# Last expert pair summed on TensorE inside the final layer norm, the last full expert unit moved ahead, and every low part of an expert weight made by VectorE

## The chip, the cores and the metric

The kernel runs on one core of one Trainium2 chip. The metric is device time in microseconds (us), from launch to end. A core has five engines with queues of their own: TensorE (PE in the rows, its weight loads PEld), VectorE (DVE), ScalarE (ACT), GpSimd (POOL) and SyncE (SP, which here only issues transfers). Each works through its queue in order, and semaphores tie the queues together.

## The reference

Two blocks of a model follow each other on 1024 tokens of width 1024. The change touches the end of the second: a mixture of 16 experts and the layer norm behind it.

```python
def grouped_moe(x, router_w, router_bias, w_gate, w_up, w_down):
    scores = jax.nn.sigmoid((xt @ router_w).astype(jnp.float32))
    # each token: the best group of experts, in it TOP_K = 2 experts, gates normalised
    ...
    def expert_block(args):
        xb, ei = args
        hb = jax.nn.silu(xb @ w_gate[ei]) * (xb @ w_up[ei])
        return hb @ w_down[ei]
    ...
    y = (yb[dest].reshape(T, TOP_K, D) * gate[..., None].astype(x.dtype)).sum(1)

# second_block, at its end
        ff = grouped_moe(x, router_w, router_bias, w_gate[l], w_up[l], w_down[l])
        x = layer_norm(DEEPNORM_ALPHA * x + ff, ln_moe_g[l], ln_moe_b[l])
```

## The kernel before

Tokens lie in eight tiles of 128 rows. After the cross attention each finished tile is stored three times (`tile`): as it is for the later gathers (`x2`, `x2a`), and times ALPHA into `acc`, a table in HBM on which the experts' results are added. `router` takes two tiles at a time: a long chain of small VectorE instructions picks the experts and counts rows, with a few TensorE products between (L2294 counts, L2368 places rows), and `table_a` and `table_b` write the row numbers for the gathers.

The experts' work comes in units (`experts`). A full unit (`full`, m = 0 to 15, here F0 to F15) gathers up to 128 rows of one expert, turns them, and multiplies in split precision: each fp32 matrix is cut into a high part (ScalarE, L2398) and a low part (L2401), and `mm3` makes three one-pass products (L336 to L338) of them. A half unit (`half`, H0 to H15) takes 64 further rows of an expert in plain fp32 (L2514 first matrix, L2538 second). Two half units share a gather and one result tile `yB`; H14 and H15 form the last pair, P7, H12 and H13 form P6. Every full unit and every pair ends in an indirect transfer from GpSimd's queue that adds its rows onto `acc` (L2379); these adds follow one another (`self.added`), since two of them may touch the same row.

An expert's weights are six tiles of 512 KB. Four go into general slots. The last two (`w` in the rows), those of the second matrix, go into a ring of two buffers for every expert but 0, 1 and 15: the next expert's two can be loaded only when full and half unit of this expert are done with them. So F14 and H14 wait for a load that itself waits for H13.

The order of all this is made by `Plan.run`: each step has an engine, a cost, a key and dependencies, and is issued to the engines' queues in the order in which the plan would start it. A step may name two engines; the plan takes the one that would end it sooner. The low part of a weight is such a step (`("dve", "pool"), (1.14, 2.3)` in `split`). Of 102 low parts 91 stand on VectorE and 11 on GpSimd.

When the plan is done, `rest` handles overflow (a loop that is not entered with these inputs). `finish_all` then loads the eight tiles of `acc` (L2705), all behind the last add, and norms them one after the other: mean and variance on VectorE (tiles 0, 2, 4, 6) or in two ScalarE passes (L2718, L2719; tiles 1, 3, 5, 7), the root on GpSimd, the rest on VectorE (L2730, L2739) or on ScalarE and GpSimd (L2736, L2737), and a store (L2740).

Of the kernel before, what the change touches and what calls it, by code (L numbers as in the profile page):

```python
# [9 lines left out]
F32 = mybir.dt.float32  # L10
F32R = mybir.dt.float32r
# [10 lines left out]
D = 1024  # L22
NT = 8
# [168 lines left out]
class K:  # L192
    def __init__(self, tc, nc, ctx, A):
        self.tc, self.nc, self.A = tc, nc, A
        P = lambda name, bufs, **k: ctx.enter_context(tc.tile_pool(name=name, bufs=bufs, **k))
        self.cp = P("const", 1)
        self.sp = P("slots", 41)
        self.xp = P("x", 3)
        self.wp = P("wts", 2)
        self.mp = P("small", 4)  # L200
        self.pp = P("psum", 2, space=PSUM)
# [294 lines left out]
def L(f, *a):  # L496
    return lambda *x: f(*a, *x)
# [1638 lines left out]
class Moe:  # L2136
# [253 lines left out]
    def split(self, plan, key, raw, W, c, slot, deps=(), room=()):  # L2390
        k, nc = self.k, self.k.nc

        def hi():
            if slot:
                W[c] = k.slot([128, 1024], F32R, "mh"), k.slot([128, 1024], F32R, "ml")
            else:
                W[c] = tuple(k.wp.tile([128, 1024], F32R, tag=t, name=k.nm(t)) for t in ("wh", "wl"))
            nc.scalar.copy(W[c][0], raw[c])  # L2398

        def lo(e):  # L2400
# [89 lines left out]
    def half(self, plan, key, m, x, raw, B, got, ready, done):  # L2490
# [76 lines left out]
        if v:  # L2567
            self.added = plan.op("pool+", 1.46, key, lambda: self.add(self.tb[0][:, p:p + 1], b0.pop("y")), b0["o"] + [self.added],
                                 free=["sl"])

    def table(self, acc, w, lo, hi, out):
        V, n = self.k.nc.vector, hi - lo
# [41 lines left out]
    def experts(self, plan, ld):  # L2614
# [61 lines left out]
        def norm():  # L2676
            self.fin = k.bcast(k.A["ln_moe_g"], D), k.bcast(k.A["ln_moe_b"], D)
        plan.op("sp+", 2.9, 126, norm, [began[13]], ["sl", "sl"])

    def blocks(self, plan, d):  # L2680

# [15 lines left out]
        plan.op("dve", 0.6, 110, count, [d], free=["pt"])  # L2697

    def finish_all(self, out):
        k = self.k  # L2700
        self.rest()
        ys, Z = {}, {}
        for i in range(NT):
            ys[i] = k.slot([128, 1024], name="fin")
            k.nc.sync.dma_start(out=ys[i], in_=self.acc[i * 128:(i + 1) * 128, :])  # L2705
        for i in range(NT + FIN_LAG):
            if i < NT:
                Z[i] = self.center(ys[i], i)
            if i >= FIN_LAG:
                self.finish(*Z.pop(i - FIN_LAG), i - FIN_LAG, out)  # L2710

    def center(self, y, i):

        k, nc, V = self.k, self.k.nc, self.k.nc.vector
        r, z = k.small([128, 1], "rstd"), k.slot([128, 1024], name="z")
        if i in FIN_ACT:
            mean, var = k.small([128, 1], "fs"), k.small([128, 1], "fv")
            nc.scalar.activation(z, y, AF.Copy, scale=-1.0 / D, accum_out=mean)  # L2718
            nc.scalar.activation(z, y, AF.Square, bias=mean, accum_out=var)  # L2719
            nc.gpsimd.tensor_scalar(r, var, 1.0 / D, LN_EPS, op0=OP.mult, op1=OP.add)  # L2720
            nc.gpsimd.tensor_tensor(r, r, k.mhalf[:, :1], op=OP.pow)
            op = OP.add
        else:
            st, mv = k.small([128, 2, 6], "bn"), k.small([128, 2], "mv")
            for h in range(2):
                V.bn_stats(st[:, h, :], y[:, h * 512:(h + 1) * 512])
            V.bn_aggr(mv, st.rearrange("p a b -> p (a b)"))
            k.rsqrt(r, mv[:, 1:2], LN_EPS)
            mean, op = mv[:, 0:1], OP.subtract
        V.scalar_tensor_tensor(z, y, mean, self.fin[0], op0=op, op1=OP.mult)  # L2730
        return z, r

    def finish(self, z, r, i, out):
        nc = self.k.nc
        if i in FIN_POOL:
            nc.scalar.activation(z, z, AF.Copy, scale=r)  # L2736
            nc.gpsimd.tensor_add(z, z, self.fin[1])  # L2737
        else:
            nc.vector.scalar_tensor_tensor(z, z, r, self.fin[1], op0=OP.mult, op1=OP.add)  # L2739
        nc.sync.dma_start(out=out[i * 128:(i + 1) * 128, :], in_=z)  # L2740


def build(tc, nc, A, ctx, outs, stop=None):
# [115 lines left out]
```

## Time and profile before

| what | value |
|---|---|
| time, median of 3 runs | 2333.01 us (2327.34 to 2335.35) |
| the profiled execution: its time, its span | 2338.79 us, 2337.0 us |
| busy share PE, PEld, DVE, ACT, POOL | 94%, 75%, 51%, 40%, 21% |
| mean granted TensorE clock | 0.975 |
| chain that ended last, whole span | PE 81%, DMA 7%, DVE 6%, ACT 2%, issue 2%, POOL 2% |
| the same chain, from 2050 us on, its costliest | DMA `acc<-yB,tab` 10.5%, PE L2514 9.7%, DMA `w<-w_moe` 9.6%, issue 7.4%, PE L2538 6.9%, DMA `acc<-my,tab` 5.6% |

The span is the time from the first to the last instruction; the profiled execution's own time is 1.8 us longer. [...] TensorE is nearly always busy until 2273 us and not at all from there to the end.

### The profile page before, as it was taken

What the parts mean: (1) busy time and instruction counts of PE and PEld (TensorE: products, weight loads), DVE (VectorE), ACT (ScalarE), POOL (GpSimd) and SP (SyncE); (2) the same over time, 40 slices, a digit from 0 to 9 for tenths busy, and PEclk for the clock granted to TensorE, in tenths of its full rate; (3) what the DMA queues carried; (4) which work ended last, traced back from release to release, by engine and by line L of the source; (5) the groups of instructions that cost most, each with busy time, mean ns of one, the idle gap of its engine ahead of it and who ended that gap; (6) DMA issues with size and microseconds to landing.
All of it is one profiled execution on the core that took longest, in us unless ns stands there. A gap on an engine that the chain in (4) does not pass through costs nothing.

```text
span 2337.0 us, 32698 instructions
## 1 busy us (share of the span) xinstructions
PE 2191.6 (94%) x12068; PEld 1746.3 (75%) x12068; DVE 1199.3 (51%) x2889; ACT 941.4 (40%) x1983; POOL 489.8 (21%) x629
## 2 busy tenths in 40 slices
PE   7999999999999999999999999998999998899880
PEld 7888778888777777777778898885778886666650
DVE  6323678833444444344444422787364456767544
ACT  5323677722444444444442222455101122455442
POOL 2000455300132222222300000211010013323114
PEclk9999999999999999999999999999999998999995
DMA  4112220322222221221353221229675135687855
GB/s 163 44 47 93 80 64 29 103 95 94 83 68 73 68 64 50 65 73 59 115 183 117 91 87 64 95 74 320 246 269 221 46 142 204 196 269 244 299 120 175
DMA packets 100257, 291.47 MB, mean 125 GB/s; under 512 B 12396, under 2 KB 25452, under 8 KB 100096
## 3 DMA queue, kind: packets, MB, share of 16 engines
q1 hardware_dynamic: 79072, 233.71, 28.8%
q0 software_dynamic: 6912, 25.17, 4.7%
q10 hardware_dynamic: 14112, 30.48, 4.1%
q8 instruction: 96, 1.57, 0.3%
q14 instruction: 65, 0.53, 0.1%
HBM read 206.92 MB, written 70.86 MB: 119 GB/s over the span
## 4 chain that ended last, share of the span: by engine, by line
PE 81%; DMA 7%; DVE 6%; ACT 2%; issue 2%; POOL 2%; SPq 0%; POOLq 0%; DVEq 0%; ACTq 0%
PE pd L336 15%; PE pd L338 14%; PE pd L337 14%; PE ps L336 4%; PE ps L338 4%; PE po L640 4%; PE ps L337 4%; PE ps L591 3%; PE pt L618 3%; PE pd L1898 2%; PE ps L986 2%; PE pd L2514 2%; PE po L1029 1%; DMA acc<-yB,tab 1%; DMA w<-w_moe 1%
## 5 line engine op out<-in xcount | busy, mean ns | idle before, releaser
L336 PE MATMUL pd<-fh,wh 128*128 128x512 f32 x880 | 353.7, 402 | 0.6 <-DVE st L1242 0.2
L338 PE MATMUL pd<-fh,wl 128*128 128x512 f32 x880 | 348.2, 396 | 0.5 <-DVE wl L314 0.5
L337 PE MATMUL pd<-fl,wh 128*128 128x512 f32 x880 | 347.7, 395 | 0.0
L336 PE MATMUL pd<-wh,fh 128*128 128x258 f32 (+3 forms) x616 | 202.0, 328 | 2.1 <-DVE n L1432 2.0
L337 PE MATMUL pd<-wl,fh 128*128 128x258 f32 (+3 forms) x616 | 200.9, 326 | 0.0
L338 PE MATMUL pd<-wh,fl 128*128 128x258 f32 (+3 forms) x616 | 200.5, 326 | 0.0
L336 PEld LDWEIGHTS pd<-fh,wh 128*128 128x128 f32 x880 | 165.4, 188 | 42.9 <-issue 7.1
L338 PEld LDWEIGHTS pd<-fh,wl 128*128 128x128 f32 x880 | 165.4, 188 | 40.0 <-issue 2.3
L337 PEld LDWEIGHTS pd<-fl,wh 128*128 128x128 f32 x880 | 165.6, 188 | 34.9 <-issue 0.2
L314 DVE TENSOR_TENSOR wl<-w,wh 128x1024 fp32r<-128x1024 f32 (+5 forms) x92 | 106.7, 1165 | 138.6 <-ACT wh L312 138.6
L312 ACT CAST wh<-w 128x1024 fp32r<-128x1024 f32 (+5 forms) x99 | 97.2, 990 | 140.9 <-PE pd L337 111.6
L626 ACT COPY PT<-pt 128x512 f32<-128x512 f32 (+2 forms) x192 | 86.3, 478 | 139.5 <-PE pt L618 139.1
L605 POOL TENSOR_SCALAR P<-P,rinv 128x256 f32<-128x256 f32 (+7 forms) x128 | 95.7, 748 | 192.8 <-DVE rinv L604 163.1
L602 ACT ACTIVATE P<-P,m 128x256 f32<-128x256 f32 (+7 forms) x128 | 99.6, 778 | 76.8 <-DVE m L596 75.7
L336 PEld LDWEIGHTS pd<-wh,fh 128*128 128x128 f32 x616 | 116.4, 189 | 13.3 <-DVE n L1432 2.7
L337 PEld LDWEIGHTS pd<-wl,fh 128*128 128x128 f32 x616 | 116.4, 189 | 9.9 <-issue 0.2
L338 PEld LDWEIGHTS pd<-wh,fl 128*128 128x128 f32 x616 | 116.3, 189 | 9.9
L1305 POOL TENSOR_TENSOR dm<-lcb,mask 128x128 f32<-128x128 f32 x128 | 60.4, 472 | 282.1 <-DVE m L596 227.3
L591 PE MATMUL ps<-st,st 128*128 128x512 f32 (+3 forms) x384 | 106.4, 371 | 1.0 <-DMA st<-st 0.6
L640 PE MATMUL po<-PT,V 128*64 128x256 f32 (+1 forms) x640 | 95.8, 371 | 0.0
L618 PE MATMUL pt<-ident,P 128*128 128x128 f32 x576 | 88.4, 276 | 3.6 <-POOL P L605 3.3
L596 DVE CUSTOM_DVE_ANT_0 P<-ps,lcb 128x512 f32<-128x512 f32 (+3 forms) x112 | 63.8, 570 | 48.3 <-PE ps L591 47.6
(499 smaller groups left out, 4730.9 us busy)
## 6 DMA issues: line engine op xcount, KB each, us to landing
mw<-w_moe SPq DMA_DIRECT2D x70, 512.0 KB, 7.0
w<-o_wc SPq DMA_DIRECT2D x30, 512.0 KB, 4.1
w<-w_moe SPq DMA_DIRECT2D x26, 512.0 KB, 5.1
xr<-xs SPq DMA_DIRECT2D x18, 512.0 KB, 4.6
s<-x_wkv SPq DMA_DIRECT2D x16, 512.0 KB, 5.7
lcb<-dn SPq DMA_DIRECT2D x16, 512.0 KB, 4.6
st<-st ACTq DMA_DIRECT2D x64, 128.0 KB, 2.4
wkd<-kvw SPq DMA_DIRECT2D x32, 256.0 KB, 2.7
```

What stands on the lines that cost most here:

```text
L312: nc.scalar.copy(hi[:, :n], raw[:, :n])
L314: (eng or nc.vector).tensor_sub(lo[:, :n], raw[:, :n], hi[:, :n].bitcast(F32))
L336: first = mm(out, lhs[0], rhs[0], start=start, stop=False)
L337: mm(out, lhs[0], rhs[1], start=False, stop=False)
L338: mm(out, lhs[1], rhs[0], start=False, stop=stop)
L591: ins = nc.tensor.matmul(ps[:, :m], l, r, start=t == 0, stop=t == len(passes) - 1)
L596: nc.vector.tensor_tensor_reduce(sb[:, c0:c0 + n0], ps[:, c0 - c:c0 - c + n0], b, -scale, acc, OP.add, OP.min, mx)
L602: nc.scalar.activation(sb[:, :w], sb[:, :w], AF.Exp, bias=acc, scale=-1.0, accum_out=sm)
L605: nc.gpsimd.tensor_scalar(sb[:, :w], sb[:, :w], ri, 0.0, op0=OP.mult, op1=OP.add)
L618: ins = nc.tensor.transpose(pt[:, j * 128:(j + 1) * 128], p[:, (c + j) * 128:(c + j + 1) * 128], k.ident)
L626: nc.scalar.copy(dst, src)
L640: st["V", n + i] = nc.tensor.matmul(o[a * 64:(a + 1) * 64, cols], val(a, j), PT[i // 2, a, j // 4][:, j % 4, n0:], start=j == 0, stop=j == ...
```

## The change

1. `finish_all` no longer finds the last pair in `acc`. P7's result `yB` stays on the chip (`self.last`), and the plan has no add for it. A new step `choose` builds `sel`, a matrix of ones and zeros that says which of its rows belongs to which token. `finish_all` cuts `yB` into high and low part, and for each of the eight tiles TensorE sums in PSUM: the identity times the loaded `acc` tile in plain fp32 (`sums`), and `sel` times the two parts (`pair`).
2. The norm reads that sum from PSUM. Only tile 0 takes its statistics from VectorE; tiles 1 to 7 take two ScalarE passes each. VectorE centres every tile (out of PSUM) and finishes it; GpSimd only makes the roots. The steps are ordered by a plan of their own, with room for four tiles in PSUM.
3. `MT_ORDER`: F15 stands ahead of H13, not behind it.
4. All low parts go to VectorE (cost 1.2 in the plan), none to GpSimd. As one step's cost and engine change, the plan issues everything behind the first of them in another order.

```diff
-MT_ORDER = ... [(v, m + 1 - v) for m in range(2, 15) for v in range(2)] + [(1, 15)]
+MT_ORDER = MT_ORDER[:-4] + [(0, 15), (1, 13), (1, 14), (1, 15)]
...
-FIN_ACT, FIN_POOL, FIN_LAG = (1, 3, 5, 7), (0, 1, 2, 4), 1
+FIN_ACT = range(1, 8)
...
-            (nc.vector, nc.gpsimd)[e].tensor_sub(W[c][1], raw[c], W[c][0].bitcast(F32))
+            nc.vector.tensor_sub(W[c][1], raw[c], W[c][0].bitcast(F32))
...
-        return plan.op(("dve", "pool"), (1.14, 2.3), key, lo, [d])
+        return plan.op("dve", 1.2, key, lo, [d])
...
+        if m == 15:
+            plan.op("-", 0, key, lambda: b0.update(last=b0.pop("y")), b0["o"])
+            self.last = b0
+        elif v:
             self.added = plan.op("pool+", 1.46, key, lambda: self.add(...), b0["o"] + [self.added], free=["sl"])
...
+    def choose(self):
+        ...
+        V.tensor_tensor(self.sel.rearrange("p (i t) -> p i t", i=8), self.iota.unsqueeze(1).to_broadcast([128, 8, 128]),
+                        t[:, 8:16].unsqueeze(2).to_broadcast([128, 8, 128]), op=OP.is_equal)
...
+        def sums(i):
+            PS[i] = banks.tile([128, 1024], F32, tag="sum", name=k.nm("sum"))
+            for n in range(2):
+                nc.tensor.matmul(PS[i][:, s(n)], k.ident, fin[i][:, s(n)], start=True, stop=False)
+        def pair(i, n):
+            for w in (yh, yl):
+                nc.tensor.matmul(PS[i][:, s(n)], self.sel[:, i * 128:(i + 1) * 128], w[:, s(n)], start=False, stop=w is yl)
+        def mean(i):
+            nc.scalar.activation(junk, PS[i], AF.Copy, scale=-1.0 / D, accum_out=T[i][0])
+        def var(i):
+            nc.scalar.activation(junk, PS[i], AF.Square, bias=T[i][0], accum_out=T[i][1])
+        def center(i):
+            V.scalar_tensor_tensor(Z[i], PS.pop(i), T[i][0] if i in FIN_ACT else T[i][:, 0:1], self.fin[0], ...)
+        def last(i):
+            V.scalar_tensor_tensor(Z[i], Z[i], R[i], self.fin[1], op0=OP.mult, op1=OP.add)
```

Where instructions stand now. First GpSimd's queue around the router of tiles 4 and 5 (`ml` and `wl` are low parts, `rstd` roots of the attention's norm, `xg` gathered rows), before:

```order
L370 TENSOR_TENSOR rstd_17478<-rstd_17478,mhalf 128x1
L2401 TENSOR_TENSOR ml_17590<-mw_17537,mh_17589 128x1024
L2401 TENSOR_TENSOR ml_17626<-mw_17539,mh_17625 128x1024
L2401 TENSOR_TENSOR ml_17629<-mw_17555,mh_17628 128x1024
L2401 TENSOR_TENSOR wl_17665<-mw_17584,wh_17664 128x1024
L369 TENSOR_SCALAR rstd_17724<-mv_17722 128x1
```

and VectorE's queue behind that router now (`rt` are the router's last small steps, `ptl` and `xr` belong to the attention, `tab` is the table for the gathers):

```order
L2367 TENSOR_TENSOR rt_17553<-rt_17553 128x4x24
L2072 TENSOR_TENSOR ptl_17643<-pt_17644,pth_17642 128x512
L2072 TENSOR_TENSOR ptl_17643<-pt_17657,pth_17642 128x512
L2404 TENSOR_TENSOR ml_17590<-mw_17537,mh_17589 128x1024
L2404 TENSOR_TENSOR ml_17625<-mw_17539,mh_17624 128x1024
L2088 SCALAR_TENSOR_TENSOR xr_17453<-xr_17453,pd_17665 128x512
L2375 TENSOR_TENSOR mcst_16088<-mcst_16088,po_17416 128x48
L2591 TENSOR_SCALAR tab_17731<-mcst_16088 128x16
```

The subtractions that stood on GpSimd while VectorE did the router's steps stand on VectorE behind those steps.

TensorE's queue at the end of the experts, before (weights `w_20088` belong to expert 13, `w_20147` to 14; the row of `w_19984` is H12, the `mid_20113` and `mid_20141` rows are H14 and H15, the `pd` rows their first matrix; `ps_20149` is F13, `ps_20168` F15, `ps_20215` F14):

```order
L2538 MATMUL ps_20074<-w_19984,mid_19804 64x512 x2
...
L2514 MATMUL pd_20083<-mw_19605,xbT_20037 64x256 x4
...
L2538 MATMUL ps_20136<-w_20088,mid_19843 64x512 x2
...
L336 MATMUL ps_20149<-wh_20121,ms_19875 128x512
...
L336 MATMUL ps_20168<-mh_19955,ms_20079 128x512
...
L2538 MATMUL ps_20200<-w_20147,mid_20113 64x512 x2
...
L2538 MATMUL ps_20206<-mw_19806,mid_20141 64x512 x2
...
L336 MATMUL ps_20215<-wh_20177,ms_19990 128x512
```

and now (`ps_20088` is F13, `w_19999` with `mid_19919` H13, `pd_20127` the first matrix of H14, `ps_20181` F15, `ps_20199` F14):

```order
L339 MATMUL ps_20088<-wh_20053,ms_19961 128x512
...
L2541 MATMUL ps_20119<-w_19999,mid_19919 64x512 x2
...
L2517 MATMUL pd_20127<-mw_19693,xbT_20079 64x256 x4
...
L339 MATMUL ps_20181<-mh_20009,ms_20117 128x512
...
L339 MATMUL ps_20199<-wh_20159,ms_20051 128x512
...
L2541 MATMUL ps_20223<-w_20132,mid_20155 64x512 x2
...
L2541 MATMUL ps_20229<-mw_19921,mid_20179 64x512 x2
```

H13 stands ahead of the last pair's first matrix, no longer behind it, and F14 stands ahead of H14 and H15, no longer last. GpSimd's queue of adds ended, before, with F13, F14, P6, F15 and P7:

```order
L2379 DMA acc<-my_20166,tab_17739 1152x1024
L2379 DMA acc<-my_20230,tab_17739 1152x1024
L2379 DMA acc<-yB_20090,tab_17739 1152x1024
L2379 DMA acc<-my_20187,tab_17739 1152x1024
L2379 DMA acc<-yB_20211,tab_17739 1152x1024
```

and ends now, behind P5, with F13, F14, F15 and P6:

```order
L2382 DMA acc<-yB_19668,tab_17731 1152x1024
L2382 DMA acc<-my_20106,tab_17731 1152x1024
L2382 DMA acc<-my_20214,tab_17731 1152x1024
L2382 DMA acc<-my_20197,tab_17731 1152x1024
L2382 DMA acc<-yB_20001,tab_17731 1152x1024
```

One add is gone, and two full units' adds stand directly behind each other.

## Rows read from the trace of the kernel before

**Rows 1.** Four stretches: length, busy us (instructions) per engine, granted clock, DMA share, GB/s
```profile
1944.00:1950.00 6.00, 6.00 (x21) 5.34 (x22) 5.62 (x28) 2.12 (x3) 0.00 (x0) 0.50 0.00 1
1999.00:2005.00 6.00, 6.00 (x18) 4.94 (x19) 5.25 (x25) 1.33 (x2) 0.00 (x0) 0.50 0.01 3
2012.00:2225.00 213.00, 198.54 (x1148) 139.59 (x1148) 138.55 (x192) 113.81 (x174) 52.84 (x35) 0.97 0.82 259
2300.00:2337.00 37.00, 0.00 (x0) 0.00 (x0) 24.75 (x24) 13.72 (x20) 24.56 (x20) 0.50 0.57 227
```

**Rows 2.** The chain that ended last, 2246 us on: start us, us, what
```profile
2246.50 6.91 PE pd L2514 x64
2253.41 1.74 PE ps L2538 x8
2255.16 8.14 DMA w<-w_moe
2263.38 1.04 ACT wh L2398
...
2264.64 5.27 PE ps L2538 x16
2269.91 0.43 PE ps L336
...
2272.95 0.76 DVE my L2468
...
2274.43 6.16 DMA acc<-my,tab
...
2293.70 6.42 DMA acc<-yB,tab
...
2300.27 3.71 DMA fin<-acc
```

**Rows 3.** Timeline of TensorE near the routers: start us, us, what [idle before, releaser]
```profile
1943.98 0.61 PE L2294 MATMUL po<-rt,triu 128*128 128x16 f32 x2 [6.09 <-DVE rt L2276]
...
1998.78 0.61 PE L2294 MATMUL po<-rt,triu 128*128 128x16 f32 x2 [5.16 <-DVE rt L2276]
...
2011.83 0.64 PE L2446 MATMUL pt<-ident,mid 128*128 128x128 f32 x2 [3.34 <-DVE xl L2422]
```

**Rows 4.** VectorE's groups, 1880 to 2280 us: count | busy us, mean ns | idle
```profile
L2401 DVE TENSOR_TENSOR wl<-w,wh 128x1024 fp32r<-128x1024 f32 x26 | 31.2, 1220 | 15.5 <-ACT wh L2398 15.4
...
L2272 DVE TENSOR_TENSOR rt<-rt 128x32 f32<-128x32 f32 x6 | 8.4, 1400 | 0.2
L2269 DVE TENSOR_TENSOR rt<-rt 128x32 f32<-128x32 f32 x6 | 7.0, 1162 | 0.2
...
L2274 DVE SCALAR_TENSOR_TENSOR rt<-rt 128x32 f32<-128x32 f32 x3 | 2.7, 901 | 0.1
```

**Rows 5.** Two of those small router steps in VectorE's timeline
```profile
1943.51 0.19 DVE L2272 TENSOR_TENSOR rt<-rt 128x32 f32<-128x32 f32 x1
...
1991.82 5.33 DVE L2272 TENSOR_TENSOR rt<-rt 128x32 f32<-128x32 f32 x1
```

**Rows 6.** GpSimd beside the second of them, in its timeline
```profile
1992.43 4.66 POOL L2401 TENSOR_TENSOR ml<-mw,mh 128x1024 fp32r<-128x1024 f32 x2
```

**Rows 7.** GpSimd's low parts by line: ns min/median/max, first and last start
```profile
L2401 POOL TENSOR_TENSOR ml<-mw,mh x10: 2338/2400/2985, 1933.5 to 2152.3; 128x1024 fp32r<-128x1024 f32 x10
```

**Rows 8.** Plain fp32 products, 128 by 128 by 512, in TensorE's timeline
```profile
1610.17 1.88 PE L1929 MATMUL po<-s,kv 128*128 128x512 f32 x4
1611.89 1.88 PE L1929 MATMUL ps<-s,kv 128*128 128x512 f32 x4
```

**Rows 9.** ScalarE's two passes over tile 1 in its timeline, first and last row
```profile
2305.34 1.06 ACT L2718 ACTIVATE z<-fin 128x1024 f32<-128x1024 f32 x1 [33.11 <-DVE bn L2726]
...
2307.58 0.19 ACT L2719 ACTIVATION_READ_ACCUMULATOR z<-fin,fs 128x1 f32 x1
```

**Rows 10.** VectorE's last instruction in its timeline
```profile
2332.01 1.29 DVE L2739 SCALAR_TENSOR_TENSOR z<-z,rstd,s 128x1024 f32<-128x1024 f32 x1 [0.44 <-POOL rstd L2721]
```

**Rows 11.** The stores by issue: count, KB each, median us to landing
```profile
out<-z SPq DMA_DIRECT2D x8, 512.0 KB, 2.6
```

More of the change, by code (lines that the diff above doesn't have):

```diff
@@ L200, in __init__ @@
         self.mp = P("small", 4)
-        self.pp = P("psum", 2, space=PSUM)
+        self.pctx = ExitStack()
+        self.pp = self.pctx.enter_context(tc.tile_pool(name="psum", bufs=2, space=PSUM))
+        self.pool = lambda name, bufs, **o: ctx.enter_context(tc.tile_pool(name=name, bufs=bufs, **o))
         self.dp = P("dram", 1, space=DRAM)
@@ L2398, in hi, with lo @@
             nc.scalar.copy(W[c][0], raw[c])
[L2400 to L2401 removed]
+        def lo():
+            nc.vector.tensor_sub(W[c][1], raw[c], W[c][0].bitcast(F32))
         d = plan.op("act", 0.95, key, hi, deps, room)
[L2403 removed]
+        return plan.op("dve", 1.2, key, lo, [d])
     def full(self, plan, key, x, at, W, got=None, ready=(None,) * 6, frees=((), ())):
@@ L2566, in half @@
         b0["o"].append(plan.op("dve", 0.6, key, L(out, 1), [b0["o"][-1]], free=["ps"]))
-        if v:
+        if m == 15:
+            plan.op("-", 0, key, lambda: b0.update(last=b0.pop("y")), b0["o"])
+            self.last = b0
+        elif v:
             self.added = plan.op("pool+", 1.46, key, lambda: self.add(self.tb[0][:, p:p + 1], b0.pop("y")), b0["o"] + [self.added],
                                  free=["sl"])
+    def choose(self):
+        k, V = self.k, self.k.nc.vector
+        self.sel, t = k.slot([128, 1024], F32R, "sel"), self.cst[:, 656:680]
+        V.tensor_scalar(t[:, 0:1], self.rowid, 2.0, -2046.0, op0=OP.mult, op1=OP.add)
+        V.tensor_add(t[:, 0:1], t[:, 0:1], self.pt[:, 23:24])
+        V.tensor_scalar(t[:, 8:16], self.tok, -1.0, t[:, 0:1], op0=OP.mult, op1=OP.add)
+        V.tensor_tensor(self.sel.rearrange("p (i t) -> p i t", i=8), self.iota.unsqueeze(1).to_broadcast([128, 8, 128]),
+                        t[:, 8:16].unsqueeze(2).to_broadcast([128, 8, 128]), op=OP.is_equal)
     def table(self, acc, w, lo, hi, out):
@@ L2678, in experts @@
         plan.op("sp+", 2.9, 126, norm, [began[13]], ["sl", "sl"])
+        plan.op("dve", 1.6, 116, self.choose, [tb, began[12]], ["sl"])
     def blocks(self, plan, d):
@@ L2699, in finish_all @@
     def finish_all(self, out):
-        k = self.k
+        k, nc, V = self.k, self.k.nc, self.k.nc.vector
         self.rest()
-        ys, Z = {}, {}
-        for i in range(NT):
[L2704 to L2740, printed above, removed]
+        k.pctx.close()
+        banks = k.pool("sums", 4, space=PSUM)
+        y, fin, Z, R, T, PS = self.last["last"], {}, {}, {}, {}, {}
@@ new lines, in finish_all, with load, hi, lo @@
+        yh, yl, junk = k.slot([128, 1024], F32R, "yh"), k.slot([128, 1024], F32R, "yl"), k.slot([128, 1024], name="junk")
+        s = lambda n: slice(n * 512, (n + 1) * 512)
+        def load(i):
+            fin[i] = k.slot([128, 1024], name="fin")
+            nc.sync.dma_start(out=fin[i], in_=self.acc[i * 128:(i + 1) * 128, :])
+        def hi(n):
+            nc.scalar.copy(yh[:, s(n)], y[:, s(n)])
+        def lo(n):
+            V.tensor_sub(yl[:, s(n)], y[:, s(n)], yh[:, s(n)].bitcast(F32))
@@ new lines, in var, with stats, root @@
+        def var(i):
+            nc.scalar.activation(junk, PS[i], AF.Square, bias=T[i][0], accum_out=T[i][1])
+        def stats(i):
+            T[i] = k.ln_stats(PS[i])[0]
+        def root(i):
+            R[i] = k.small([128, 1], "rstd")
+            if i in FIN_ACT:
+                nc.gpsimd.tensor_scalar(R[i], T[i][1], 1.0 / D, LN_EPS, op0=OP.mult, op1=OP.add)
+                nc.gpsimd.tensor_tensor(R[i], R[i], k.mhalf[:, :1], op=OP.pow)
+            else:
+                k.rsqrt(R[i], T[i][:, 1:2], LN_EPS)
@@ new lines, in center @@
+        def center(i):
+            Z[i] = k.slot([128, 1024], name="z")
+            V.scalar_tensor_tensor(Z[i], PS.pop(i), T[i][0] if i in FIN_ACT else T[i][:, 0:1], self.fin[0],
+                                   op0=OP.add if i in FIN_ACT else OP.subtract, op1=OP.mult)
+        def last(i):
+            V.scalar_tensor_tensor(Z[i], Z[i], R[i], self.fin[1], op0=OP.mult, op1=OP.add)
+        plan = Plan(2.0, bk=4)
+        parts = []
+        for n in range(2):
+            d = plan.op("act", 0.57, -1, L(hi, n))
+            parts.append(plan.op("dve", 0.66, -1, L(lo, n), [d]))
@@ new lines, in finish_all @@
+        for i in range(NT):
+            d = plan.op("sp+", 1.46, i, L(load, i))
+            d = plan.op("pe", 1.72, i, L(sums, i), [d], ["bk"])
+            for n in range(2):
+                d = plan.op("pe", 0.46, i - 0.5, L(pair, i, n), [d, parts[n]])
+            if i in FIN_ACT:
+                d = plan.op("act", 1.24, i, L(mean, i), [d])
+                v = plan.op("act", 1.34, i, L(var, i), [d])
+            else:
+                d = v = plan.op("dve", 1.6, i, L(stats, i), [d])
+            r = plan.op("pool", 1.2, i, L(root, i), [v])
+            d = plan.op("dve", 1.28, i, L(center, i), [d])
+            plan.op("-", 0, i, lambda: None, [v, d], free=["bk"])
+            d = plan.op("dve", 1.28, i, L(last, i), [d, r])
+            plan.op("sp+", 1.46, i, lambda i=i: nc.sync.dma_start(out=out[i * 128:(i + 1) * 128, :], in_=Z.pop(i)), [d])
@@ L2743, in build @@
+        with k.tc.manual_schedule(engines=SW_MAN):
+            plan.run()
 def build(tc, nc, A, ctx, outs, stop=None):
```

2 lines of the change are left out of this document (added).

## Prediction

> **What bounds the kernel now.** I read the page first for the shares, then the table of busy time by stretch, then the chain that ended last, then TensorE's waits, and at last the timelines of the engines around the longest of these waits. In the long middle of the experts TensorE is busy 198.5 of 213 us while the DMA engines are at 0.82 [rows 1]: that part is bound by TensorE's work, with 14.5 us of idle time in it. The end is bound otherwise. The chain [rows 2] goes from H13's second matrix (to 2255.15) to the load of expert 14's last two weight tiles (8.14), their split, the second matrices of H14, H15 and last of F14, F14's result, and then four adds onto the table, one behind the other, until the tiles of `acc` can be loaded at 2300.27. From there 36.7 us go to the norm, in which TensorE does nothing [rows 1]. Ahead of the long middle there is a third place: twice TensorE waits over 5 us for the router's small VectorE steps [rows 3].
>
> **The change, part by part.**
>
> *One add less.* Between the first and the last of the four adds of the tail and the load stand 2300.27 - 2274.43 = 25.8 us for four, 6.46 each [rows 2]. The last pair is not added any more, and the three others (F14, F15, P6) still follow one another: -6.5. What P7 costs instead lies beside the adds: its split by ScalarE and VectorE and the last four products come while GpSimd adds, some 19 us long. The matrix `sel` costs VectorE one large instruction (1024 elements, as the 1.22 of a low part [rows 4]) and three small ones, in a queue that is busy 138.6 of 213 us there [rows 1]; nothing.
>
> *F14 ahead of H14 and H15.* Expert 14's weights land at 2255.16 + 8.14 = 2263.30 and F14's add begins 11.1 us later, since sixteen instructions of the two half units stand ahead of F14's twelve [rows 2]. Now F14 stands ahead: cast 1.04, subtraction 1.22 with some 0.1 of hand-over, twelve products 2272.95 - 2269.91 = 3.0, result and issue 2274.43 - 2272.95 = 1.5 [rows 2, 4]; sum 6.9. That is -4.2. Should TensorE come to these twelve at its lower level, 3.0 of it is lost. I don't expect that: between H13 and F14 it now has H14's and H15's first matrix (6.9) and F15's twelve products (3.0), 9.9 us against 8.14 + 2.4 = 10.5 for load and split, so it stands still for half a microsecond.
>
> *H13 earlier.* The load for expert 14 starts when H13 is done. Before, the 6.91 us of the last pair's first matrix stood ahead of H13 and F13's 3.0 behind it [rows 2]; now it is the other way round: -3.9, if expert 13's weights are there in time (zero if they come just that much later, which the plan's order does not show).
>
> *The norm out of PSUM.* I count from the issue of the first load of `acc`. The first tile lands after 3.7 [rows 2]. For each tile TensorE has two plain fp32 products of 512 columns, which are four instructions: start to start, four such took 1611.89 - 1610.17 = 1.72 [rows 8]; and four one-pass products at 0.25 (3.0 over twelve), 1.0. So 2.7 a tile, 21.8 for eight. TensorE has been idle for some 20 us by then, and after both waits of rows 3 its clock stood at 0.50 for 6 us of full work [rows 1]. I take the same here: 6 us that do the work of 3. Last product at 3.7 + 6 + 18.8 = 28.5. ScalarE's two passes over a tile took 2307.77 - 2305.34 = 2.43 [rows 9], a little less than TensorE's 2.7, so it ends one tile behind: 30.9. In the built program VectorE's centring of a tile waits for ScalarE's second pass over it, and behind the last centring stand the finish of tile 6 and of tile 7: three instructions of 1.29 [rows 10], 3.8, to 34.7. The last store lands 2.6 after its issue [rows 11], and the span ended 1.1 after the landing in the kernel before (2333.3 + 2.6 to 2337.0): 38.5. The norm before took 36.7, so this part costs +1.8. Four tiles of room in PSUM hold nothing up: a tile's room is free some 7 us behind its last product, and TensorE comes back to it after 8. Bounds: clock back after half of that time, +0.3; TensorE at 0.50 all the way, 3.7 + 43.6 + 2.4 + 3.8 + 2.7 + 1.1 = 57.3, that is +20.6.
>
> [...]
>
> *Low parts on VectorE.* On GpSimd one takes 2.4 [rows 7], on VectorE 1.22 [rows 4]. But the small router steps tell more: L2272 takes 0.19 alone and 5.33 beside two subtractions of GpSimd, and ends with them [rows 5, 6]. Over the fifteen steps of L2269, L2272 and L2274 the busy time is 18.1 where 15 times 0.19 would be 2.9 [rows 4, 5]: 15.2 us by which the two routers' ends came late. TensorE's waits for them, 6.1 and 5.2 [rows 3], would go whole, and with them the two stretches at the lower clock, 3.0 each [rows 1]: 17.3 in all. Against it: eleven subtractions, 13.4 us, join VectorE's queue. The first two stand behind the router's steps, ahead of an addition of the attention; two more than before come ahead of the `xl` for which TensorE waited 3.3 already [rows 3], 2.4 later. 17.3 - 2.4 = 14.9. I take two thirds, 10: the middle is bound by TensorE, so time won ahead of it lasts, but its new order of 213 us has transfers at 0.82 and 14.5 us of idle time that may grow as well as shrink. Bounds: 20 gained (the 17.3 and most of the third wait in rows 3), and 6 lost (none of it won, and idle time in the middle up by 6 of its 14.5).
>
> *Sum.* -6.5 - 4.2 - 3.9 + 1.8 - 10 = -22.8. The profiled execution took 2338.8 (a span of 2337.0 and 1.8 around it): 2316.0. It is 5.8 above the median of the runs shown; from that median, 2333.0, the same difference gives 2310.
>
> **The rivals.**
>
> *Only the tail gains.* What the routers no longer lose comes back as waits for weights or rows in the middle. For it: transfers are at 0.82 there, and the plan's order differs in every queue. Against: only 14.5 us of idle time stood there. 2333.0 - 12.8 = 2320.
>
> *TensorE's clock does not come back in the norm.* It stands at 0.50 when the sums begin [rows 1]. Then the norm costs +20.6 and the sum is -4.0: 2329. For it: 36 us in which TensorE is paced by others could keep it low. Against: it is not paced, having 2.7 a tile where ScalarE needs 2.4, and after full work in rows 1 the level rose.
>
> *VectorE becomes the bound of the first experts (slower).* Place: the first full units, around the second router. The subtractions that stood on GpSimd there now stand in one queue with the attention's norm and the router's second chain, and TensorE needs each before it may go on. If all eleven, 13.4, fall into TensorE's way, and three waits of that kind each bring a stretch at the lower clock (3.0 each), this costs 22.4 in place of the gain of 10: 2333.0 - 12.8 + 22.4 = 2343. It decides from 12.8 on, that is when ten of the eleven are on TensorE's path. Against: while GpSimd subtracted, VectorE's small steps stood still anyway.
>
> *All of it.* The routers' 17.3 and most of the third wait are won, and the norm's clock is back early: 2333.0 - 14.6 + 0.3 - 20 = 2299.
>
> **How the numbers follow.** Forecast 2310, with 6 in 10; only the tail 2 in 10; no clock in the norm 0.07; all of it 0.07; VectorE the bound 0.06. Faster by over 0.3% (7 us, about what a measurement of this kernel can tell from no change) means below 2326: the first, second and fourth, less a little for a forecast that misses both terms: 0.87. Same: 0.07. Slower: 0.06. The range of 8 in 10 leaves out the two ends: 2297 to 2326.
>
> **What the profile would show.** Three adds between F14's result and the loads, 6.5 apart. F14's add some 7 us behind the landing of its weights. Router steps L2269, L2272 and L2274 (by their new numbers) at 0.2 each, and no wait over 5 us of TensorE for `rt`. In the norm, TensorE at 0.50 for its first two tiles and at 1.00 behind, then one tile each 2.7 us; last store some 38 us behind the first load. I would be wrong if TensorE's idle time between 1950 and 2250 grew by more than 10 us, if a weight load ended later against the work around it, or if the sums ran at 0.50 to the end.

## The result and the profile after

The changed kernel took 2303.5 us (median of 4 runs, 2300.9 to 2306.6), the kernel before beside it 2334.2: a ratio of 0.9876 (95% interval 0.9860 to 0.9891). Measured once more later, it took 2307.4 beside 2329.9: 0.9897 (0.9881 to 0.9914). So the change brings 22 to 31 us; the forecast was 2310 and 22.8 us less. It is faster, and inside the range given.

The profiled execution has a span of 2304.8 us, 32.2 less than the one of before. That one lies 5.8 above its own median and the one of after 3.1 above its own, so differences between the two traces read some 3 us too large. It shows where: the first router's count of rows already stands 2.8 earlier (1823.94, before 1826.72), ahead of all that is compared here.

The stretches that answer to [rows 1]: columns are length, busy us (instructions) of PE, PEld, DVE, ACT, POOL, then the granted clock, the DMA share and GB/s. The long middle now begins 20 us earlier (a wait that ended at 2011.83 ends at 1991.82).

```profile
1944.00:1950.00 6.00, 6.00 (x28) 4.88 (x27) 5.16 (x10) 0.00 (x0) 3.21 (x4) 1.00 0.32 91
1960.00:1965.00 5.00, 2.46 (x8) 2.17 (x9) 4.40 (x5) 3.34 (x5) 4.50 (x3) 0.50 0.47 122
1990.00:1995.00 5.00, 3.18 (x9) 2.60 (x10) 5.00 (x8) 1.32 (x2) 0.00 (x0) 0.50 0.57 200
1992.00:2205.00 213.00, 196.41 (x1104) 134.70 (x1106) 139.56 (x194) 113.06 (x169) 50.30 (x34) 0.97 0.80 246
2268.00:2305.00 37.00, 23.63 (x64) 13.06 (x64) 21.41 (x19) 16.25 (x28) 5.88 (x16) 0.82 0.57 227
2272.00:2276.00 4.00, 4.00 (x7) 1.91 (x6) 0.00 (x0) 0.00 (x0) 0.00 (x0) 0.50 1.03 417
```

The stretch at the lower clock (0.50) at 1944 is gone, and TensorE now works at 0.50 in two stretches there, at 1960 and 1990. The kernel before had four: the two of [rows 1] and these two, behind shorter waits of TensorE (2.9 and 2.2 us at the first, 3.3 ahead of the second):

```profile
1976.00:1981.00 5.00, 3.83 (x12) 3.17 (x13) 3.54 (x4) 2.00 (x2) 1.90 (x1) 0.50 0.64 174
2012.00:2015.00 3.00, 3.00 (x9) 2.43 (x9) 3.00 (x3) 1.31 (x2) 1.79 (x1) 0.50 1.01 328
```

The middle has 16.6 us of idle time where [rows 1] had 14.5. In the norm TensorE is busy 23.6 us in place of none, and its clock is back at 2276.

What the routers' stretch gained in all can be read between two marks, a router's product of scores (L2217, now L2220) and the end of the wait at 2011.83, now 1991.82. TensorE has 301 recorded instructions between them in both kernels; before and after:

```profile
1927.44:2011.83 84.39, 62.97 (x301) 52.20 (x300) 62.91 (x148) 28.69 (x41) 31.82 (x20) 0.86 0.55 196
1924.94:1991.82 66.88, 55.43 (x301) 46.90 (x299) 56.04 (x156) 28.53 (x41) 12.79 (x11) 0.93 0.76 267
```

That is 17.5 us less: 10.0 less of waiting, and 7.5 less for the same work, at the higher clock (0.93 in place of 0.86 on the mean).

The timeline of TensorE near the second and third router, as in [rows 3] (start us, us, what, idle before and its releaser):

```profile
1935.24 0.37 PE L2297 MATMUL po<-rt,triu 128*128 128x16 f32 x2
1962.54 1.11 PE L2211 MATMUL pt<-ident,xr 128*128 128x128 f32 x4 [4.49 <-DVE xl L2425]
1978.29 0.38 PE L2297 MATMUL po<-rt,triu 128*128 128x16 f32 x2
1991.82 0.69 PE L2449 MATMUL pt<-ident,mid 128*128 128x128 f32 x2 [5.33 <-DVE xl L2425]
```

The two counts stand at 1935.24 and 1978.29 where [rows 3] has 1943.98 and 1998.78, and without a wait. In their place TensorE waits twice, 4.5 and 5.3 us, for `xl` (the low part of a full unit's turned rows). The timelines ahead of the second of these waits show why: ScalarE had `xh`, which `xl` needs, done by 1987.2, but in VectorE's queue low parts of weights stand ahead of `xl`.

```profile
1986.09 1.07 ACT L2422 CAST xh<-pt 128x512 fp32r<-128x512 f32 x2
```

```profile
1988.81 2.35 DVE L2404 TENSOR_TENSOR ml<-mw,mh 128x1024 fp32r<-128x1024 f32 x2
1991.08 1.28 DVE L2425 TENSOR_TENSOR xl<-pt,xh 128x512 fp32r<-128x512 f32 x2
```

VectorE's groups from 1858 to 2260 us (count | busy us, mean ns | idle), to be set beside [rows 4]; L2272, L2275 and L2277 are the steps that were L2269, L2272 and L2274:

```profile
L2404 DVE TENSOR_TENSOR wl<-w,wh 128x1024 fp32r<-128x1024 f32 x26 | 31.5, 1223 | 13.2 <-ACT wh L2401 12.9
...
L2272 DVE TENSOR_TENSOR rt<-rt 128x32 f32<-128x32 f32 x6 | 1.2, 194 | 0.2
L2275 DVE TENSOR_TENSOR rt<-rt 128x32 f32<-128x32 f32 x6 | 1.2, 193 | 0.2
L2277 DVE SCALAR_TENSOR_TENSOR rt<-rt 128x32 f32<-128x32 f32 x3 | 0.6, 194 | 0.1
```

Fifteen steps take 3.0 us in place of 18.1. The chain that ended last, where [rows 2] had H13, the weights and four adds:

```profile
2232.35 1.87 PE ps L2541 x8
2234.22 6.91 PE pd L2517 x64
...
2248.43 6.15 DMA acc<-my,tab
...
2261.28 6.04 DMA acc<-yB,tab
2267.45 3.78 DMA fin<-acc
2271.36 3.75 PE sum L2740 x4
```

H13 ends at 2234.22, F14's add begins 14.2 us later (19.3 before), the loads 19.0 behind that (25.8 before: four adds then, three now), and from the first load to the end of the span go 37.35 us (36.7 before). The load of expert 14's weights is no longer in this chain. Its second tile is there 5.0 us behind H13's end, where [rows 2] has 8.1, and TensorE comes to F14 later than that, straight from F15's products:

```profile
2239.25 1.05 ACT L2401 CAST wh<-w 128x1024 fp32r<-128x1024 f32 x1 [0.32 <-DMA w<-w_moe]
```

```profile
2243.96 0.39 PE L339 MATMUL ps<-wh,ms 128*128 128x512 f32 x1
```

Last, ScalarE and VectorE near the end of the norm:

```profile
2295.09 1.02 ACT L2749 ACTIVATE junk<-sum 128x1024 f32<-128x1024 f32 x1 [0.27 <-PE sum L2745]
```

```profile
2297.48 1.28 DVE L2767 SCALAR_TENSOR_TENSOR z<-sum,fs,s 128x1024 f32<-128x1024 f32 x1 [0.15 <-ACT junk L2752]
2298.68 2.47 DVE L2771 SCALAR_TENSOR_TENSOR z<-z,rstd,s 128x1024 f32<-128x1024 f32 x2
```

ScalarE waits 0.27 us for TensorE's sums ahead of its tile, and the same ahead of the tiles before: the norm is paced by TensorE's 2.64 us a tile. Behind the last pass stand three VectorE instructions, as the prediction had it.

### The profile page after: what moved, and what is told of

It reads as the page before. It is cut to its first block, busy times and chain, and to the rows that moved or that the text cites. A ratio compares the mean times of both kernels' runs of the same rounds, so it can differ in the third digit from the quotient of the medians.

```text
span 2304.8 us, 32807 instructions
## 1 busy us (share of the span) xinstructions
PE 2205.0 (96%) x12132; PEld 1749.5 (76%) x12132; DVE 1193.1 (52%) x2902; ACT 946.9 (41%) x1992; POOL 445.1 (19%) x613
## 4 chain that ended last, share of the span: by engine, by line
PE 81%; DVE 6%; DMA 6%; ACT 2%; issue 2%; POOL 1%; SPq 0%; DVEq 0%; ACTq 0%; POOLq 0%
PE pd L339 15%; PE pd L341 15%; PE pd L340 15%; PE po L643 4%; PE ps L339 4%; PE ps L341 4%; PE ps L340 4%; PE ps L594 3%; PE pt L621 3%; PE pd L2517 2%; PE pd L1901 2%; PE ps L989 2%; DMA acc<-my,tab 1%; PE po L1032 1%; DMA mw<-w_moe 1%
## 5 line engine op out<-in xcount | busy, mean ns | idle before, releaser
L2404 DVE TENSOR_TENSOR ml<-mw,mh 128x1024 fp32r<-128x1024 f32 x66 | 79.7, 1220 | 19.3 <-ACT mh L2401 12.0
```

Of the source, the lines that this page charges most:

```text
L2404: nc.vector.tensor_sub(W[c][1], raw[c], W[c][0].bitcast(F32))
```

## The experiments

The theory: the low parts on GpSimd held up the small steps of the routers on VectorE, and this, an add less and the earlier F14 make up the gain. The main rival: the gain comes from the new order that the plan makes of everything. Each kernel was measured in five rounds beside the kernel before; ratios are to that kernel on the same chip.

**Part 4 taken back.** The changed kernel with

```diff
-            nc.vector.tensor_sub(W[c][1], raw[c], W[c][0].bitcast(F32))
+            (nc.vector, nc.gpsimd)[e].tensor_sub(W[c][1], raw[c], W[c][0].bitcast(F32))
...
-        return plan.op("dve", 1.2, key, lo, [d])
+        return plan.op(("dve", "pool"), (1.14, 2.3), key, lo, [d])
```

> The changed kernel with part 4 alone taken back: a low part may go to GpSimd again (1.14 on VectorE, 2.3 on GpSimd), and the plan orders everything anew. Theory (GpSimd's subtractions hold up the small VectorE steps of the routers, and TensorE waits for these): the 17 us by which H13's end came earlier beyond its new place are lost, so 2303.5 + 17 = 2320, at least 2313; the steps of 128x32 again take up to 4 or 5 us beside GpSimd's subtractions, and TensorE's waits for rt over 5 us are back. Rival (the gain ahead of the long middle is owed to the new order of the full and half units, F15 and F14 moved, not to who subtracts): within 4 us of the changed kernel, 2299 to 2308.

Measured: 2324.7, a ratio of 0.9973 (0.9964 to 0.9982). Parts 1 to 3 alone bring only 6.3 us, and part 4 on top of them 18 (by the second measurement of the changed kernel) to 23 (by the first). VectorE's groups of the routers (1858 to 2270 us) and TensorE's waits:

```profile
L2275 DVE TENSOR_TENSOR rt<-rt 128x32 f32<-128x32 f32 x6 | 8.4, 1404 | 0.2
...
L2274 DVE TENSOR_REDUCE rt<-rt 128x2 f32<-128x32 f32 x6 | 1.1, 187 | 0.2
```

```profile
PE po L2297 <- DVE rt L2279: 11.0, 2, 5.8
```

Most steps with two inputs are slow again (0.5 to 1.4 us on the mean), the reductions between them (one input, 0.19) never were, and both waits for `rt` are back. The rival is out.

**Part 4 alone.** The kernel before with the same two lines changed the other way (as in the diff of the change).

> The kernel before with part 4 alone: all low parts on VectorE, cost 1.2, everything else as before. Theory: the 17 us come with this edit alone: 2334 - 17 = 2317, and no more than 2324; the router's small steps are at 0.2 us each. Rival (the order of the last units carries part of it): less than half of that, 2326 or above. If the routers' steps are at 0.2 and the time is still 2326 or above, the time comes back as another wait.

Measured: 2319.4, a ratio of 0.9948 (0.9933 to 0.9962), 12 us less than before. The steps are at 0.19 and the waits for `rt` gone, so the theory holds, but alone the part is worth 12 and not 17.

**The old order, all on VectorE.** The kernel before, its plan untouched, one line changed:

```diff
-            (nc.vector, nc.gpsimd)[e].tensor_sub(W[c][1], raw[c], W[c][0].bitcast(F32))
+            nc.vector.tensor_sub(W[c][1], raw[c], W[c][0].bitcast(F32))
```

> The kernel before, its plan and with it the order on every engine left alone, but the eleven subtractions that stood on GpSimd are issued on VectorE, at the same place of the program. Theory (the hold-up by GpSimd costs VectorE more than the subtractions themselves): in the routers of tiles 4 to 7 15.2 us of hold-up go, and about seven subtractions of 1.2 (8.5) come into the same stretch; TensorE's two waits for rt get shorter by 2 to 4 us each: 2334 - 6 = 2328, between 2322 and 2332. Rival (VectorE is simply loaded with 13.4 us more, with no hold-up to win): 2334 to 2347. If it is as fast as the changed plan with part 4 alone, the plan's new order has no part in the gain.

Measured: 2320.6, a ratio of 0.9957 (0.9943 to 0.9972), which can't be told from part 4 alone. By the ratio that is 10 us. So what brings the 10 to 12 us is who subtracts; the order that the plan makes behind it adds nothing that can be measured. My own figure, 6, was too small: I had counted what the steps lose, less what the subtractions cost, but part of these must fall where VectorE or TensorE would have waited anyway; which part, no run shows. TensorE's waits from 1880 to 2260 us (total, times, longest):

```profile
PE pt L2446 <- DVE xl L2422: 9.0, 3, 4.6
...
PE po L2368 <- DVE rt L2364: 2.3, 3, 1.6
```

Of 11.2 us of waiting for `rt` at the counts none is left; the wait for `xl` went from 7.6 to 9.0.

**An idle GpSimd made busy.** The changed kernel, with subtractions that nobody needs in every router:

```diff
         def choose(j):
+            if j == 0:
+                q = B["t"][:, 704:1008].rearrange("p (a b) -> p a b", a=2)
+                for _ in range(7):
+                    nc.gpsimd.tensor_sub(q, *[flat(B["sc"])[:, 0:2].unsqueeze(2).to_broadcast([128, 2, 152])] * 2)
...
```

> The changed kernel, and in each of the four routers GpSimd gets seven subtractions of 128x304 whose result nobody reads (some 0.7 us each, 5 us in all), started just ahead of the router's choosing steps; GpSimd is idle there otherwise. Theory: the 128x32 steps of VectorE beside them stand still until GpSimd is done, 3 to 5 us a router, though no data tie them together; where TensorE has no other work for that long it waits for rt: 3 to 12 us slower, 2307 to 2316. Rival (the long steps of before were VectorE waiting for something else, such as a semaphore or data): the steps stay at 0.2 us and the time within 2 us of the changed kernel.

Measured: 2309.9, a ratio of 0.9910 (0.9896 to 0.9925): by the ratios 3 to 8 us slower than the changed kernel, too little to be told from its second measurement. The trace decides. GpSimd's seven in a router, and VectorE's steps beside them:

```profile
1971.77 5.45 POOL L2273 TENSOR_TENSOR rt<-rt 128x304 f32<-128x304 f32 x7 [8.40 <-DVE rt L2252]
```

```profile
1973.13 0.17 DVE L2260 TENSOR_TENSOR rt<-rt 128x8 f32<-128x8 f32 x1
1973.33 0.68 DVE L2261 TENSOR_TENSOR rt<-rt,mcst 128x8 f32<-128x8 f32 x1
1974.05 0.16 DVE L2262 TENSOR_REDUCE rt<-rt 128x2 f32<-128x8 f32 x1
1974.25 0.54 DVE L2263 TENSOR_TENSOR rt<-rt 128x8 f32<-128x8 f32 x1
1975.27 0.34 DVE L2276 TENSOR_TENSOR rt<-rt 128x32 f32<-128x32 f32 x1
```

One GpSimd instruction lasts 5.45 / 7 = 0.78 on the mean, so by estimate they end at 1972.55, 1973.33, 1974.11, 1974.89 and 1975.67; the held steps end at 1974.01, 1974.79 and 1975.61, each within 0.1 of one of these ends. No data tie the two together. That is the hold-up itself. Its size I had wrong: one short instruction holds a step up for 0.5 at most, some 1.6 us in a router over all its steps, where I expected 3 to 5. The long subtractions of 2.4 us, two of which kept the step of [rows 5] for 5.33 us in place of 0.19, are what made it dear.

**The changed kernel again**, to stand on one chip with the next three.

> The changed kernel once more, to stand on the same chip as the three others: 2303, within 4 us.

Measured: 2307.4 (2302.9 to 2310.5), a ratio of 0.9897 (0.9881 to 0.9914), with a span of 2304.9; that is 0.4 outside the 4 us expected.

**Part 3 taken back.** The line on `MT_ORDER` is left out.

> The changed kernel without part 3: F15 stands behind H13 again. Theory (the load of expert 14's last two tiles waits for H13, and F14's add for that load): H13 and the load come 3.9 us later, and F14's sixteen instructions of H14 and H15 stand ahead of it again, 4.2: 2303 + 8 = 2311, between 2308 and 2314. Rival (the order of two units moves transfers in the middle, and these outweigh it): outside this range on either side. Rival (the adds one behind the other set the end, whatever the units' order): 2303 to 2306.

Measured: 2310.0, a ratio of 0.9907 (0.9891 to 0.9923). That is 2.6 more than the changed kernel, and not to be told from it; the profiled span is 4.6 longer (2309.5). In this trace H13 ends 2.4 us later, and F14's add begins 16.2 behind it, not 14.2: the plan has put F14 ahead of H14 and H15 here too, without the line. So the line is worth some 4 and not 8, if anything.

**Parts 1 and 2 taken back.** The changed kernel with P7's add and the old `finish_all`:

```diff
-        if m == 15:
-            plan.op("-", 0, key, lambda: b0.update(last=b0.pop("y")), b0["o"])
-            self.last = b0
-        elif v:
+        if v:
...
```

> The changed kernel without parts 1 and 2: P7 is added onto the table by GpSimd and the norm is that of the kernel before. Theory: one add more, 6.45, and a norm of 36.7 in place of 37.4: 2303 + 5.8 = 2309, between 2307 and 2312. Rival (a fourth add hides behind the units, since F14's add is the only one that is late): 2301 to 2304, no slower than the changed kernel.

Measured: 2314.7, a ratio of 0.9931 (0.9917 to 0.9946), 7.3 more than the changed kernel on that chip. The last two adds, in GpSimd's timeline:

```profile
2261.29 1.56 POOL L2380 DMA_INDIRECT acc<-yB,tab  x1 [4.80 <-DMA acc<-my,tab]
2268.33 1.56 POOL L2380 DMA_INDIRECT acc<-yB,tab  x1 [5.49 <-issue]
```

The loads begin at 2274.75 where the changed kernel has 2267.90 (6.85 later), and the norm takes 37.25 us against 37.0. The time is above the 2307 to 2312 expected, since the changed kernel itself stood at 2307.4 here; the difference, 7.3 where I expected 5.8, is a little more than expected.

**Pair products first.** The order within a sum turned round, and the four tiles for which the norm's plan has room in PSUM started before the loads:

```diff
-                nc.tensor.matmul(PS[i][:, s(n)], k.ident, fin[i][:, s(n)], start=True, stop=False)
+                nc.tensor.matmul(PS[i][:, s(n)], k.ident, fin[i][:, s(n)], start=False, stop=True)
...
+            if n == 0:
+                PS[i] = banks.tile([128, 1024], F32, tag="sum", name=k.nm("sum"))
             for w in (yh, yl):
-                ... start=False, stop=w is yl)
+                ... start=w is yh, stop=False)
...
```

> The changed kernel with the order of the sums turned round: for the four tiles that PSUM has room for, the products of sel with the last pair come ahead of the loads of acc, while TensorE stands idle for 20 us; the identity times the loaded tile comes last. Theory (TensorE's 2.64 us a tile paces the norm, not ScalarE's 2.43): behind the load the first four tiles take 1.72 each, ScalarE's seven tiles of 2.43 or VectorE's eight of 2.56 become the pace, and TensorE has its clock when the first tile comes: 2303 - 5 = 2298, between 2296 and 2300. Rival (the norm is paced by ScalarE and VectorE anyway): within 1.5 us of the changed kernel. Rival (TensorE's clock is down again by the time the first tile lands): 1 to 3 us less gain than the theory, 2299 to 2301.

Measured: 2303.3, a ratio of 0.9876 (0.9860 to 0.9893), 4.2 less than the changed kernel on that chip where the theory had 5. The two intervals overlap, so the traces have to carry it: the norm takes 34.5 us from the first load (37.0 in the changed kernel). The last rival had a share: behind 12.1 us of standing still TensorE's clock was at 0.50 until 2277.1, and sixteen instructions of the identity's products, four tiles, took 10.1 us and not 7.

```profile
2271.14 10.08 PE L2739 MATMUL sum<-fin,ident 128*128 128x512 f32 x16 [12.11 <-DMA fin<-acc]
```

**The clock kept.** The same, with 48 products that nobody reads ahead of tile 3's pair:

```diff
+            if i == 3 and n == 0:
+                for _ in range(48):
+                    nc.tensor.matmul(PS[i][:, s(n)], self.sel[:, 0:128], yh[:, s(n)], start=True, stop=True)
```

> The kernel with the pair products first, and in TensorE's idle time behind them, ahead of the first load of acc, 48 more products of 512 columns (11.3 us) whose result nobody uses: they are there only to keep TensorE busy until the first tile lands. Theory (the first two tiles of the sums run at the lower clock, 3.75 each in place of 1.72, because TensorE stood idle before them): tile 0 and tile 1 take 1.72 each, the norm ends 3 us earlier than with the pair products first alone: 2303.3 - 3 = 2300, granted clock 1.00 from the first sum on. Rival (the loads land only as fast as the first tiles are summed, 512 KB each at some 400 GB/s): 1 us or less gained, 2302 to 2304, though the clock stays up.

Measured: 2301.5, a ratio of 0.9865 (0.9849 to 0.9882). Its profiled run is 7 us faster than its three others, for reasons ahead of H13, so only the stretch behind the load is compared: 31.7 us in place of 34.5, and the same sixteen instructions take 7.1, at a granted clock of 1.00:

```profile
2264.03 7.13 PE L2739 MATMUL sum<-fin,ident 128*128 128x512 f32 x16 [1.08 <-DMA fin<-acc]
```

The 2.8 us are what the lower clock cost at the start of the norm with the pair products first. The intervals of the two kernels overlap, so the gain is shown by the trace alone.

**Two pairs.** P6 as well is kept, with a `sel` of its own, and summed on TensorE: eight products a tile, one add less.

```diff
-        if m == 15:
+        if m >= 13 and v:
             plan.op("-", 0, key, lambda: b0.update(last=b0.pop("y")), b0["o"])
-            self.last = b0
+            self.last.append(b0)
...
```

> The kernel with the pair products first, and P6 too is kept on the chip and summed on TensorE: a second matrix of ones and zeros, eight products a tile in place of four, and no add for P6. Theory (the adds follow one another and set the start of the norm, the products of four tiles lie ahead of the loads): the loads start 6.4 earlier, TensorE is busy until they land; the last four tiles take 3.6 each in place of 2.64, which costs 3 to 4 where the norm is paced by TensorE there: 2303.3 - 6.4 - 3 (clock) + 3.5 = 2297.5, between 2295 and 2300. Rival (TensorE paces the whole norm and the 1.0 more for each tile eats what the add gave): 2302 to 2306.

Measured: 2300.8, a ratio of 0.9859 (0.9842 to 0.9875), 3 more than expected. The loads begin at 2259.9, 7.5 us earlier than with one pair (1.0 of it is an earlier H13), but the norm takes 40.8. VectorE's timeline names the cause:

```profile
2260.01 2.50 DVE L2740 TENSOR_TENSOR yl<-yB,yh 128x512 fp32r<-128x512 f32 x4 [8.94 <-DMA acc<-my,tab]
```

The buffer of P6's low part was that of a row block still being added, so the products, all but the first, began at 2260.8, at the lower clock (0.60 on the mean from 2260 to 2268).

**F15's add first.** As two pairs, with F14's add issued behind F15's (it is kept back in `full` and made after F15's).

> As the one with two pairs, and GpSimd adds F15's rows ahead of F14's, since F15's result is there 2.8 us earlier. Theory: the two adds and the loads begin 2.8 us earlier, of which the norm, bound by TensorE's products from the end of the units on, gives half: 1.4 less than with two pairs, 2296. Rival (the norm waits for TensorE alone): the same as with two pairs, within 0.5. Rival (the adds set it all): 2.8 less.

Measured: 2302.7, a ratio of 0.9872 (0.9855 to 0.9888), no different from two pairs. The first add begins 1.3 earlier (2245.9), but the loads only 0.3: the second, F14's, followed 7.2 us later and not 6.5.

**Two pairs, cut ahead.** As two pairs, with P6's split ahead of P7's and the products of each part as soon as it is there:

```diff
-        for n in range(2):
-            for u in range(2):
-                d = plan.op("act", 0.57, -1, L(hi, u, n))
+        for u in range(2):
+            for n in range(2):
+                d = plan.op("act", 0.57, u - 9, L(hi, u, n))
...
```

> As with two pairs, but P6's rows are cut into high and low part first, and TensorE's products start with P6 as soon as its parts are there. In the kernel with two pairs VectorE's first low part began at 2260.01 us only, behind the last add, since its buffer was that of a row block still being added (a releaser DMA acc<-my), and TensorE's 32 products ran from 2260.8 to 2270.6 at the lower clock. Here no low part stands behind a transfer. Theory (TensorE's products are what the norm waits for): they begin at about 2254, half of them at the lower clock, and are done when the first tile lands at 2263.8; the sums then start 6.8 earlier: 2300.8 - 6.8 = 2294, between 2292 and 2297. Rival (the pace behind the landing is the same 3.56 a tile for eight tiles, whatever comes ahead): 2299 to 2302.

Measured: 2295.6, a ratio of 0.9841 (0.9826 to 0.9855): faster than the changed kernel by 8 to 13 us (by the two ratios), and its interval lies below both of that kernel's. From two pairs as they were (0.9842 to 0.9875) it can't be told by the times alone; the traces differ. TensorE's first pair product, the sums behind the load, and a stretch within these:

```profile
2257.50 0.77 PE L2751 MATMUL sum<-yh,sel 128*128 128x512 f32 x1 [2.70 <-DVEq L2601]
...
2269.85 8.83 PE L2744 MATMUL sum<-fin,ident 128*128 128x512 f32 x16 [3.01 <-DMA fin<-acc]
```

```profile
2271.00:2274.00 3.00, 3.00 (x4) 1.01 (x4) 1.41 (x3) 0.00 (x0) 0.00 (x0) 0.50 1.02 419
```

The profiled run is the slowest of its five (H13 ends at 2238.0 in it), yet its products are done by 2266.8, ahead of the first tile, and the norm takes 35.7 us against 40.8. TensorE then stood still for 3.0 us only and began the sums at 1.00, but its clock fell to 0.50 behind that, from 2271.0 to 2274.3: the sixteen instructions took 8.8 us and not 7.1.

## Why the prediction was right, and where it was off

*One add less, -6.5.* Right. Three adds stand 6.4 apart, the loads 6.85 earlier than with the pair added.

*F14 ahead and H13 earlier, -4.2 and -3.9.* Near in size together, not right in mechanism. F14's add stands 5.1 nearer to H13's end, but 3.1 of these are the load, 5.0 us in place of 8.1, which the prediction took as fixed; only 1.9 are the order. The add begins 9.2 behind the weights, not 7: F14's products waited for F15's on TensorE and not for load and split. So a shorter load made up for what the order did not give, and that is luck; why it was shorter, no run shows. The kernel with the old order and all on VectorE, where H14 and H15 still stand ahead of F14, has the add only 15.4 behind H13 with its load of 5.5. Of the 3.9 for H13's place 0.9 is left: from 1991.82 to H13's end it is 242.4 us where it was 243.3 (from 2011.83 on); the middle's idle time there grew by 1.5. And the order was put down to the wrong edit: part 3 alone is worth 2.6 by the medians, 4.6 by the spans, and the kernel with part 4 alone also has F14 ahead, its add 15.7 behind H13's end. I read the new order from a plan in which both edits stood, and gave it to one.

*The norm out of PSUM, +1.8.* The mechanism as described (TensorE 2.64 a tile, ScalarE right behind it, three VectorE instructions at the end); it came to +0.3 to +0.6 over [rows 1]'s norm, and to nothing beside the old norm of the kernel with the pair added (37.25). From the first sum to the last product it is 23.6 us where I had 24.8: eight tiles of 2.64 are 21.1 and not 21.8, and the clock was back after 4.7 us (3.8 in the second trace) and not after the 6 of [rows 1]. The rival in which it never returns is excluded.

*Low parts on VectorE, -10.* Right in mechanism; the third taken off was too much for this trace. The routers' stretch gained 17.5 where the prediction counted 14.9 ahead of taking two thirds; by the times part 4 brings 10 to 12 alone and 18 to 23 on top of the other parts. Both waits for `rt` went, 11.2 us. What the prediction set against it came too: TensorE waits for `xl` 12.6 us at L2449 and L2211, where before it was 7.6 at L2446, and two stretches at 0.50 follow these waits. But they take the place of four, two of which I had not counted. The slower rival named this place rightly; its price, 22.4, was not paid: 5.0 more of waiting for `xl`, and no stretch at the lower clock more than before.

*What the profile would show.* Three adds, router steps at 0.2, no wait over 5 us for `rt` and 2.64 us a tile came as forecast; F14's add 9.2 us behind its weights did not.

*The hold-up itself.* In the kernel before the six steps of L2272, which have two inputs, took 1.40 us on the mean [rows 4], now 0.19; the reductions between them (L2268 and L2271) took 0.18 and 0.19 in that kernel too. The held steps end within 0.1 us of the ends of GpSimd's instructions. But they do not all wait for one instruction. The 5.33 of [rows 5] lasts through two subtractions of GpSimd standing back to back [rows 6], though it began 0.6 us ahead of the first of them, while GpSimd issued a transfer. And beside the router of tiles 4 and 5 two steps did end between GpSimd's subtractions, while the next was held for two of them; VectorE and GpSimd before:

```profile
1933.70 2.30 DVE L2272 TENSOR_TENSOR rt<-rt 128x32 f32<-128x32 f32 x1
1936.03 2.32 DVE L2274 SCALAR_TENSOR_TENSOR rt<-rt 128x32 f32<-128x32 f32 x1
...
1938.61 4.42 DVE L2269 TENSOR_TENSOR rt<-rt 128x32 f32<-128x32 f32 x1
```

```profile
1933.51 7.17 POOL L2401 TENSOR_TENSOR ml<-mw,mh 128x1024 fp32r<-128x1024 f32 x3 [11.23 <-ACT mh L2398]
1940.56 2.41 POOL L2401 TENSOR_TENSOR wl<-mw,wh 128x1024 fp32r<-128x1024 f32 x1
...
1991.44 0.97 POOL L2376 DMA_INDIRECT xg<-x2a,tab  x1 [0.16 <-issue]
```

What decides between the two, no run shows.

*The sum.* -22.8 stands between the two measurements, -30.7 and -22.5. Between the two traces, from the mark at 1927.44 on, the terms are -17.5 (routers), -0.9 (H13), -5.1 (F14), -6.8 (adds) and +0.6 (norm): the forecast came near partly because errors of both signs stood in it. Taken one after the other, part 4, then part 3, then parts 1 and 2, the ratios give 12, 4 and 8 us, which is 24. In the other order parts 1 to 3 give 6 and part 4 then 18. That the tail gains less while GpSimd still subtracts stays partly open: in that kernel F14's add comes 1.9 later behind H13 and the norm takes 0.5 to 0.9 more, which leaves some 3 us without a place, and a difference of ratios is no surer than that.

## What to carry to other kernels

A step of 0.2 us that takes 5 is the thing to look for: set the timeline of the engine beside it next to it, and if it ends when that engine's instruction ends, move that instruction, even where it makes the busier queue longer (part 4 alone brought 10 to 12 us). While the last adds followed one another here, TensorE stood idle for 20.3 us, until the first tile had landed, so sums that need no transfer belong there: they took work from the path (the norm took 34.5 us with the pair products first, 37.0 without) and, where they lasted until 1.1 us ahead of the data (the kernel with the clock kept), the clock stood at 1.00 through the sums. And see that no buffer of that work is still held by the transfers it is to hide behind: with two pairs one was, and the norm took 40.8 us, with the pairs cut ahead 35.7.

## What the runs showed of the hardware

Short GpSimd instructions held VectorE up far less than long ones: seven of 0.78 us cost a router 1.6 us, while two of 2.4 back to back cost 5.1 in one step [rows 5, 6]. TensorE's clock, after 20.3 and 20.7 us of standing still, was at 0.50 for 4.7 and 3.8 us of full work in the norm of the changed kernel's two traces, and for 6.0 in the kernel with the pair products first, behind 12.1 us of standing still. Products ahead of the load did not prevent this by themselves: in the kernel with two pairs cut ahead it fell to 0.50 during the sums, behind a wait of 3.0. With the 48 more products, and a wait of 1.1, it stayed at 1.00 through the sums, and four tiles' identity products took 7.1 us in place of 10.1; so it did in the kernel with two pairs, where the products ran on into the sums without a wait (7.0). The last adds, from F14's or F15's on, began 6.1 to 7.2 us apart.
